# Token shift, wide products and low parts off GpSimd, PSUM banks freed earlier, and fewer small transfers in a two-layer GLA / MoBA / RWKV-7 step

## The chip, the cores and the metric

The kernel runs on one core of a Trainium2 chip. A core has four compute engines with an instruction queue each: TensorE (PE in the profile, with its weight loads as PEld), VectorE (DVE), ScalarE (ACT) and GpSimd (POOL). A fifth queue, SyncE (SP), only issues DMA transfers. Each queue runs in order and waits on semaphores. The metric is the device time of one execution in microseconds; lower is better.

## The reference

Two layers of a hybrid decoder trunk run on 256 prompt tokens and 8 single-token samples (264 columns in all), with 1024 features. Per layer:

```python
gq, gk, gv, g_low, g_out, mq, mk, mv, pr, pg = split_cols(x @ p['w_in'], IN_SPLITS)
# GLA branch: chunked linear attention, gated with silu(g_out)
# MoBA branch: rotary on mq, mk; softmax attention over own and cached blocks
prev = jnp.concatenate([shift0[:, None, :], pr[:, :-1]], axis=1)      # RWKV-7 branch: token shift
ps = pr + p['rwkv_mu'] * (prev - pr)
r, k7, v7, w_low, a_low, gr_low = split_cols(ps, RWKV_SPLITS)
...
k7 = k7 * (1.0 + (a - 1.0) * p['rwkv_k_a'])
yw, wkv_S = rwkv7_scan(r, w, k7, v7, kk, a, wkv_S0)                   # done in chunks of 64 tokens
...
merged = sum over branches of sigmoid(pg + b_gate) * (branch @ w_branch)
x = layer_norm(ALPHA * x + merged @ p['w_out'], ln1_g, ln1_b)
h = jnp.square(relu(x @ p['w_up'])) @ p['w_down']
x = layer_norm(ALPHA * x + h, ln2_g, ln2_b)
```

The caches and recurrent states are returned as well.

## The kernel before

Activations lie feature-major: 128 features on the partitions, 264 tokens along a row, 8 such row tiles for the 1024 features. All dense weights stream through in 146 chunks of 512 KB per layer (`Weights`, L206 to L241). A chunk is loaded into one of three staging tiles (`st`) from the SP queue; ACT casts it to a reduced-precision high part `wh`, DVE subtracts to get the low part `wl` (`split`, L200 to L202). `unit` (L283) takes one chunk and issues 24 matmuls of 128x264: high by high, high by low, low by high. So PE needs from ACT and DVE two casts and two subtractions of 128x512 for each 24 matmuls. `next` cuts a chunk two units ahead of its use and asks for loads further ahead.

In a layer the units run in this order: the RWKV projections `pr` (14 row tiles, collected in four groups `prp`, then shifted by `tok_shift` into `pst`, L643), GLA's `gq gk gv go`, MoBA's `mq mk` with rotary (`rope`, L1280) and `mv`, the gates and branch products for GLA, RWKV and MoBA, then `w_out` with LN1, 32 units of `w_up`, and `w_down` with LN2. The three branches are Python generators (`rwkv`, `gla`, `moba`, and `samples` for the RWKV sample states) that are advanced between units, so that their small work stands between the dense matmuls. The order on each engine is then fixed at build time by a scheduler with a simulated timeline; at run time each queue follows that order and waits where it must.

Places and names that the change and the prediction touch:

- `tok_shift(g)` (L643 to L653): GpSimd forms the difference of neighbouring columns of `prp` for a whole group (128x1024), DVE applies `mu` and adds, row by row.
- `rwkv`: `k7` gets its affine part on DVE (L713) and its product with `kx` on GpSimd (L718); `bk` and `qr` (decayed keys and queries, L741 to L745) are half DVE, half GpSimd. `parts` (L603) makes high and low parts of `rk` and `ys`, the low part on GpSimd (L606).
- `Dg` to `Mb` and `Tb` to `TZ`: 16x16 diagonal blocks are inverted with blocks on partitions. Two transposing round trips through DRAM re-arrange them: `md` (write L766, eight reads L769) and `td` (write L883, sixteen reads L887). PE's products `y` (L900) need `Zt`, which is made from `TZ` (L896). `S<-in_wkv` (L824) are two loads of the samples' states, `sa` (PE) reads them.
- `emit_go` (L1273 to L1276) gates GLA's output: ACT's tanh and a DVE product read the PSUM bank of the unit. `rope` (L1280 to L1292): ACT copies the bank to SBUF, then three ACT and one DVE copy of 32 partitions read the bank again, crosswise. Ordinary units have two PSUM banks in turn, so a bank that is held delays the unit after the next.
- `LayerNorm`: `prepare` scales the residual with alpha (L418), `add` adds the products. After LN1's statistics (`rs`, L505) early `w_up` units, computed without normalisation, are fixed up: DVE `u` (L479), GpSimd `u * rs` (L481), ACT relu (L1523), GpSimd square (L1525). Mode "keep" (LN1) also writes the normalised rows `s` for the next residual: GpSimd subtracts `mu` (L515) and multiplies by `rs` (L519), DVE applies gain and bias (L520), and later ACT multiplies by alpha (L418).
- `quad` (L185): a set of small matmuls of which the last is issued first, the others after it.

Of the kernel before, what the change touches and what calls it, by code (L numbers as in the profile page):

```python
# [10 lines left out]
F32 = mybir.dt.float32  # L11
# [10 lines left out]
NS = 8  # L22
# [89 lines left out]
def kernel(ctx: ExitStack, tc: tile.TileContext, i, o, depth):  # L112
# [72 lines left out]
    def quad(products):  # L185

        out, l, r, start, stop = products[-1]
        head = PE.matmul(out, l, r, start=start, stop=stop).ins
        with tc.issue_after(head):
            for out, l, r, start, stop in products[:-1]:  # L190
                mm(out, l, r, start, stop)
# [13 lines left out]
    class Weights:  # L205
# [27 lines left out]
        def next(self):  # L233
            c = self.used
            self.used += 1
            ahead = NWP // 2 - 1
            self.cut_to(c + ahead)
            self.load_to(c + ahead + NST)
            return self.pc.pop(c)
# [158 lines left out]
    class LayerNorm:  # L398
# [16 lines left out]
        def prepare(self, m):  # L415
            s = self.s[ALL, m]
            if isinstance(self.x, Rows):
                A.mul(s, s, alpha)  # L418
            else:
                A.mul(s, self.x.h.f32(m), alpha)  # L420
                V.scalar_tensor_tensor(s, self.x.l.f32(m), alpha, s, op0=OP.mult, op1=OP.add)
            if m > 2:
                G.tensor_tensor(s, s, self.k, op=OP.subtract)

        def add(self, m, ps):
            s = self.s[ALL, m]
            V.tensor_tensor(s, s, ps, op=OP.add)
# [63 lines left out]
        def normalise(self):  # L491
# [15 lines left out]
            if self.mode == "keep":  # L507
                for _ in range(16):
                    yield
            if self.mode == "split":  # L510
                self.xh, self.xl = Rows(KT, "xh", F32R), Rows(KT, "xl", F32R)
            for k in range(KT):
                s = self.s[ALL, k]
                e = G if self.mode == "keep" or k % 2 else V
                e.tensor_tensor(s, s, mu, op=OP.subtract)  # L515
                if self.mode == "keep":
                    yield
                    yield
# [31 lines left out]
    for l in range(depth):  # L550
# [11 lines left out]
        ka1 = lpool.tile([128, 4], F32, tag="ka1", name="ka1")  # L562
        SP.dma_start(shift0, i["shift0"][l])
# [27 lines left out]
        V.tensor_scalar(ka1, P("k_a", 0, 4), -1.0, 1.0, op0=OP.mult, op1=OP.add)  # L591
        if l == 0:
            make_idx()

        if True:
# [48 lines left out]
            def tok_shift(g):  # L644
# [4 lines left out]
                G.tensor_sub(d[:, :, 0:T], pr[:, :, 0:T], pr[:, :, 1:T + 1])  # L649
                G.tensor_sub(d[:, :, T:N], shift0[:, 4 * g:4 * g + n, :], pr[:, :, T + 1:N + 1])  # L650
                for j in range(n):
                    V.scalar_tensor_tensor(d[:, j], d[:, j], P("mu", 4 * g + j), pr[:, j, 1:N + 1], op0=OP.mult, op1=OP.add)
                G.tensor_copy(sho[:, 4 * g:4 * g + n, :], pr[:, :, T:N + 1])  # L653

            def rwkv():
# [56 lines left out]
                for m in range(4):  # L712
                    V.tensor_scalar(k7[:, m], a7[:, m], P("k_a", m), ka1[:, m:m + 1], op0=OP.mult, op1=OP.add)  # L713
# [20 lines left out]
                for hf in range(2):  # L734
# [9 lines left out]
                    G.tensor_tensor(bt[:, :, :, 64:128], v4(k7), Pi[:, hs], op=OP.mult)  # L744
                    G.tensor_tensor(qt[:, :, :, 64:128], v4(r7), Pd[:, hs, :, 1:65], op=OP.mult)  # L745
# [19 lines left out]
                md = dr.tile([8, 16, 16, 16], F32, tag="md", name="md")  # L765
                SP.dma_start(md.rearrange("b i q j -> (b i) (q j)"), Dg.rearrange("r c p j -> r (c p j)"))  # L766
# [115 lines left out]
                td = dr.tile([8, 16, 2, 16, 16], F32, tag="td", name="td")  # L882
                SP.dma_start(td.rearrange("b q z i j -> (b q) (z i j)"), Tb.rearrange("q z i j -> q (z i j)"))  # L883
# [70 lines left out]
                def pre_chunk(c):  # L954
# [3 lines left out]
                          for p in range(4) for f in HALF for h2 in range(2)])  # L958
# [142 lines left out]
            def gla():  # L1101
# [74 lines left out]
                for tt in range(2):  # L1176
# [4 lines left out]
                      for tt in range(2) for m in range(2) for a in range(2) for h2 in range(2)])  # L1181
# [128 lines left out]
            def moba():  # L1310
# [113 lines left out]
                for m in range(4):  # L1424
                    ex = []
                    pss = [bank([128, 384], "qkT") for _ in range(2)]
                    for a in range(4):
                        keys = slice(0, 128) if a < 2 else slice(0, 256)
                        cols = slice(0, 128) if a < 2 else slice(128, 384)
                        for h2 in range(2):  # L1430
                            f = HALF[h2]
                            mm(pss[h2][HALF[a % 2], cols], mq[f, m, 64 * a:64 * a + 64], mk[f, m, keys])
# [200 lines left out]
```

## Time and profile before

Three runs took 1155.83 to 1157.29 us, median 1156.64 us. One execution was profiled:

| | |
|---|---|
| time of the profiled execution | 1157.98 us |
| its span (first to last instruction) | 1156.2 us |
| PE busy / weight loads | 1086.6 us (94%) / 1014.7 us (88%) |
| DVE busy | 882.3 us (76%) |
| ACT busy | 662.0 us (57%) |
| POOL busy | 534.8 us (46%) |
| mean granted TensorE clock | 0.982 |
| DMA, mean | 166 GB/s |

Busy is the union of the spans of an engine's instructions. Matmuls overlap each other, so a busy PE may still be short of its best rate. An idle time is shown with the work whose end ended it. The granted clock is 1.00 at 2.4 GHz and 0.50 at 1.2 GHz.

### The profile page before, as it was taken

To read this page: it belongs to the slowest core of one execution; us is meant where nothing else is said; L and a number is where in the kernel's file an instruction comes from. 1 tells how busy PE (TensorE), PEld (TensorE's weight loads), DVE (VectorE), ACT (ScalarE), POOL (GpSimd) and SP (SyncE) were. 2 spreads that over 40 slices of the span, in tenths; PEclk is the share of its full clock that TensorE was granted. 3 is DMA by queue.
4 is the path that set the end of the run, shared out by engine and by line. 5 is a ranking of instruction groups with operands and counts; after the bars stand their busy time and mean duration, and the time that the engine had idled before them with its cause. 6 is when DMAs were issued, how large, how long until landed. Compare 5 with 4: busy or idle time off the path is not lost.

```text
span 1156.2 us, 26716 instructions
## 1 busy us (share of the span) xinstructions
PE 1086.6 (94%) x10284; PEld 1014.7 (88%) x10284; DVE 882.3 (76%) x1562; ACT 662.0 (57%) x1460; POOL 534.8 (46%) x633
## 2 busy tenths in 40 slices
PE   7998899999999899999989978899999998999996
PEld 7887788888999799999989867788789988999995
DVE  6898974668778998766799889555687888987554
ACT  5844444555766676655557645363567656766443
POOL 2373482460126875441265655714411377753412
PEclk9999999999999999999999989999999998999998
DMA  7445665474454455655534456645634544556661
GB/s 266 144 131 180 176 201 172 130 251 129 146 176 155 146 181 170 188 191 183 164 114 152 144 167 186 202 129 157 225 110 148 173 153 146 163 171 196 183 182 57
DMA packets 71520, 191.89 MB, mean 166 GB/s; under 512 B 21136, under 2 KB 23904, under 8 KB 71392
## 3 DMA queue, kind: packets, MB, share of 16 engines
q1 hardware_dynamic: 66240, 173.39, 47.9%
q0 software_dynamic: 5152, 16.79, 4.5%
q8 instruction: 81, 1.33, 0.5%
q14 instruction: 47, 0.39, 0.1%
HBM read 179.17 MB, written 8.88 MB: 163 GB/s over the span
## 4 chain that ended last, share of the span: by engine, by line
PE 74%; DVE 12%; issue 5%; DMA 4%; ACT 3%; SPq 1%; POOL 1%; DVEq 0%; ACTq 0%; POOLq 0%
PE ps L179 40%; PE psd L179 16%; PE psb L179 5%; DVE wl L202 4%; PE mn L179 1%; DVE s L520 1%; DMA kcache<-in_kcache,idx 1%; DMA TZ<-td 1%; DMA S<-in_wkv 1%; SPq L887 1%; ACT wh L201 1%; PE y L179 1%; PE w L183 1%; PE zy L179 1%; PE qkT L179 1%
## 5 line engine op out<-in xcount | busy, mean ns | idle before, releaser
L202 DVE TENSOR_TENSOR wl<-st,wh 128x512 fp32r<-128x512 f32 (+1 forms) x585 | 458.0, 795 | 162.2 <-ACT wh L201 155.2
L201 ACT CAST wh<-st 128x512 fp32r<-128x512 f32 (+1 forms) x585 | 354.5, 617 | 286.1 <-PE ps L179 134.0
L179 PE MATMUL ps<-xh,wh 128*128 128x264 f32 x904 | 269.4, 298 | 15.9 <-DVE go L1276 4.7
L179 PE MATMUL ps<-xl,wh 128*128 128x264 f32 x904 | 265.1, 293 | 1.8 <-DVE xl L202 1.8
L179 PE MATMUL ps<-xh,wl 128*128 128x264 f32 x904 | 264.3, 292 | 1.3 <-DVE wl L202 1.3
L179 PEld LDWEIGHTS ps<-xh,wh 128*128 128x128 f32 x904 | 174.8, 193 | 29.0 <-issue 5.5
L179 PEld LDWEIGHTS ps<-xl,wh 128*128 128x128 f32 x904 | 175.0, 194 | 6.9 <-issue 2.7
L179 PEld LDWEIGHTS ps<-xh,wl 128*128 128x128 f32 x904 | 174.9, 193 | 5.2 <-issue 2.8
L179 PE MATMUL ps<-ch,wh 128*128 128x266 f32 x600 | 174.5, 292 | 5.1 <-ACT wh L201 3.4
L179 PE MATMUL ps<-ch,wl 128*128 128x266 f32 x600 | 173.1, 290 | 6.0 <-DVE wl L202 5.9
L179 PE MATMUL ps<-cl,wh 128*128 128x266 f32 x600 | 173.4, 289 | 0.4 <-DVE cl L440 0.4
L179 PE MATMUL psd<-hh,wh 128*128 128x264 f32 x512 | 145.5, 284 | 0.0
L179 PE MATMUL psd<-hl,wh 128*128 128x264 f32 x512 | 145.3, 284 | 0.0
L179 PE MATMUL psd<-hh,wl 128*128 128x264 f32 x512 | 145.3, 284 | 0.0
L179 PEld LDWEIGHTS ps<-ch,wl 128*128 128x128 f32 x600 | 114.4, 191 | 8.1 <-DVE wl L202 7.9
L179 PEld LDWEIGHTS ps<-ch,wh 128*128 128x128 f32 x600 | 115.0, 192 | 6.6 <-ACT wh L201 3.9
L179 PEld LDWEIGHTS ps<-cl,wh 128*128 128x128 f32 x600 | 115.5, 193 | 0.9 <-DVE cl L440 0.8
L1496 POOL TENSOR_TENSOR acc<-acc,gt 128x264 f32<-128x264 f32 x32 | 35.2, 1102 | 147.8 <-DVE gt L1495 136.5
L481 POOL TENSOR_TENSOR u<-u,rs 128x264 f32<-128x264 f32 x75 | 79.2, 1056 | 37.5 <-DVE u L479 35.8
L179 PEld LDWEIGHTS psd<-hh,wh 128*128 128x128 f32 x512 | 96.4, 188 | 0.0
L179 PEld LDWEIGHTS psd<-hl,wh 128*128 128x128 f32 x512 | 96.3, 188 | 0.0
L179 PEld LDWEIGHTS psd<-hh,wl 128*128 128x128 f32 x512 | 96.3, 188 | 0.0
(598 smaller groups left out, 2167.9 us busy)
## 6 DMA issues: line engine op xcount, KB each, us to landing
st<-in_w SPq DMA_DIRECT2D x291, 512.0 KB, 3.6
S<-in_wkv SPq DMA_DIRECT2D x4, 512.0 KB, 4.8
gS<-in_gla SPq DMA_DIRECT2D x8, 256.0 KB, 5.6
out_wkvs<-S SPq DMA_DIRECT2D x4, 512.0 KB, 3.3
out_glas<-gS SPq DMA_DIRECT2D x8, 256.0 KB, 5.5
out_k<-mk SPq DMA_DIRECT2D x2, 528.0 KB, 3.7
out_v<-mv SPq DMA_DIRECT2D x2, 528.0 KB, 3.5
out_y<-s SPq DMA_DIRECT2D x8, 132.0 KB, 1.7
```

The source lines that it names most:

```text
L179: PE.matmul(out, l, r, start=start, stop=stop)
L183: PE.matmul(out, l, r, start=start, stop=stop, skip_group_check=True)
L201: A.copy(hi, src)
L202: V.tensor_sub(lo, src, hi.bitcast(F32))
L481: G.tensor_tensor(u, u, self.rs, op=OP.mult)
L520: V.tensor_scalar(s, s, self.P(self.gn, k), self.P(self.bn, k), op0=OP.mult, op1=OP.add)
L887: SP.dma_start(TZ[16 * b:16 * b + 16, z], td[b, :, z].rearrange("q i j -> i q j"))
L1496: G.tensor_tensor(acc[ALL, m], acc[ALL, m], gts[e], op=OP.add)
```

## The change

Per layer:

1. `tok_shift`: with omu = 1 - mu, the shift becomes mu * prev + omu * pr. ACT scales the neighbour columns row by row (14 operations of 128x256), DVE adds the rest (14, as before), GpSimd only copies the eight sample columns (the state is scaled with mu at the layer's start).
2. `k7`'s affine part goes from DVE to ACT, its product with `kx` from GpSimd to DVE; the GpSimd halves of `bk` and `qr` go to DVE; the low parts in `parts` go to DVE.
3. `emit_go`: ACT also takes half of the bank's value to SBUF, one DVE operation then works from SBUF. `rope`: all four crosswise copies are ACT's and read the SBUF copy.
4. LN1 "keep": gain, bias and alpha are folded (`ag`, `nag`, `ab`): two DVE operations per row tile, none on GpSimd, and no scaling by ACT in LN2's `prepare`.
5. `md` and `td`: the write makes a layout from which one read (`Mb`) and two reads (`TZ`) suffice, instead of eight and sixteen.
6. `next` asks for loads one chunk less far ahead.
7. `quad` can issue two leading matmuls, one for each of two banks; used for `mn`, `gA` and MoBA's `qkT`.

```diff
-    def quad(products):
-        out, l, r, start, stop = products[-1]
+    def quad(products, heads=1):
+        out, l, r, start, stop = products[-heads]
         head = PE.matmul(out, l, r, start=start, stop=stop).ins
+        for out, l, r, start, stop in products[len(products) - heads + 1:]:
+            with tc.issue_after(head):
+                head = PE.matmul(out, l, r, start=start, stop=stop).ins
...
-            self.load_to(c + ahead + NST)
+            self.load_to(c + ahead + NST - 1)
...
             if self.mode == "keep":
+                mr = T1([128, N], "mr")
+                V.tensor_tensor(mr, mu, rs, op=OP.mult)
                 for _ in range(16):
                     yield
+                for k in range(KT):
+                    s = self.s[ALL, k]
+                    V.scalar_tensor_tensor(s, s, ag[:, k:k + 1], rs, op0=OP.mult, op1=OP.mult)
+                    yield
+                    V.scalar_tensor_tensor(s, mr, nag[:, k:k + 1], s, op0=OP.mult, op1=OP.add)
+                    yield
+                return
...
-                A.copy(hi, src)
-                G.tensor_tensor(lo, src, hi.bitcast(F32), op=OP.subtract)
+                split(src, hi, lo)
...
-                G.tensor_sub(d[:, :, 0:T], pr[:, :, 0:T], pr[:, :, 1:T + 1])
-                G.tensor_sub(d[:, :, T:N], shift0[:, 4 * g:4 * g + n, :], pr[:, :, T + 1:N + 1])
                 for j in range(n):
-                    V.scalar_tensor_tensor(d[:, j], d[:, j], P("mu", 4 * g + j), pr[:, j, 1:N + 1], op0=OP.mult, op1=OP.add)
+                    A.mul(d[:, j, 0:T], pr[:, j, 0:T], P("mu", 4 * g + j))
+                G.tensor_copy(d[:, :, T:N], shift0[:, 4 * g:4 * g + n, :])
+                for j in range(n):
+                    V.scalar_tensor_tensor(d[:, j], pr[:, j, 1:N + 1], omu[:, 4 * g + j:4 * g + j + 1], d[:, j], op0=OP.mult, op1=OP.add)
...
-                    V.tensor_scalar(k7[:, m], a7[:, m], P("k_a", m), ka1[:, m:m + 1], op0=OP.mult, op1=OP.add)
+                    A.activation(k7[:, m], a7[:, m], AF.Identity, scale=P("k_a", m), bias=ka1[:, m:m + 1])
...
-                G.tensor_tensor(k7, k7, kx, op=OP.mult)
+                V.tensor_tensor(k7, k7, kx, op=OP.mult)
...
-                    G.tensor_tensor(bt[:, :, :, 64:128], v4(k7), Pi[:, hs], op=OP.mult)
-                    G.tensor_tensor(qt[:, :, :, 64:128], v4(r7), Pd[:, hs, :, 1:65], op=OP.mult)
+                    V.tensor_tensor(bt[:, :, :, 64:128], v4(k7), Pi[:, hs], op=OP.mult)
+                    V.tensor_tensor(qt[:, :, :, 64:128], v4(r7), Pd[:, hs, :, 1:65], op=OP.mult)
...
-                for b in range(8):
-                    SP.dma_start(Mb[16 * b:16 * b + 16], md[b].rearrange("i q j -> q i j"))
+                SP.dma_start(Mb, md.rearrange("q b i j -> (q b) i j"))
...
-                for b in range(8):
-                    for z in range(2):
-                        SP.dma_start(TZ[16 * b:16 * b + 16, z], td[b, :, z].rearrange("q i j -> i q j"))
+                for z in range(2):
+                    SP.dma_start(TZ[:, z], td[z].rearrange("q b i j -> (b i) q j"))
...
-                    V.tensor_scalar(s, s, 0.5, 0.5, op0=OP.mult, op1=OP.add)
-                    V.tensor_tensor(go[:, j], s, ps, op=OP.mult)
+                    A.mul(go[:, j], ps, 0.5)
+                    V.scalar_tensor_tensor(go[:, j], s, 1.0, go[:, j], op0=OP.add, op1=OP.mult)
...
-                    (V.tensor_copy if q == 3 else A.copy)(u[d], ps[e])
+                    A.copy(u[d], t[e, m])
```

The scheduler makes a new order from this. Three places of it follow.

POOL in layer 0, at the end of LN1: before, with `a`, `sq` the last sums of the statistics, `s` the row tiles, `u` the fix of an early unit and `hr` its square.

```order
L449 TENSOR_TENSOR sq<-sq 128x264
L450 TENSOR_TENSOR a_5006<-a_5006,s 128x264
L515 TENSOR_TENSOR s<-s,mu 128x264 x8
L481 TENSOR_TENSOR u<-u,rs 128x264
L519 TENSOR_TENSOR s<-s,rs 128x264 x8
L481 TENSOR_TENSOR u<-u,rs 128x264
```

And after the change:

```order
L453 TENSOR_TENSOR sq<-sq 128x264
L454 TENSOR_TENSOR a_5002<-a_5002,s 128x264
L485 TENSOR_TENSOR u<-u,rs 128x264
L1539 TENSOR_TENSOR hr<-hr 128x264
L485 TENSOR_TENSOR u<-u,rs 128x264
```

The sixteen operations on `s` no longer stand around the first fix on POOL.

DVE at the same place: before, from the reciprocal that gives `rs` to the third `u`.

```order
L505 RECIPROCAL rs<-rs 128x264
L202 TENSOR_TENSOR wl<-st,wh 128x512 x4
L479 SCALAR_TENSOR_TENSOR u<-mu,wgb,ps 128x264
L202 TENSOR_TENSOR wl<-st,wh 128x512
L520 TENSOR_SCALAR s<-s,prm 128x264 x2
L202 TENSOR_TENSOR wl<-st,wh 128x512
L520 TENSOR_SCALAR s<-s,prm 128x264 x2
```

And after the change, where eight operations stand in one run:

```order
L509 RECIPROCAL rs<-rs 128x264
L205 TENSOR_TENSOR wl<-st,wh 128x512
L514 TENSOR_TENSOR mr<-mu,rs 128x264
L483 SCALAR_TENSOR_TENSOR u<-mu,wgb,ps 128x264
L205 TENSOR_TENSOR wl<-st,wh 128x512
L519 SCALAR_TENSOR_TENSOR s<-s,ag,rs 128x264 x8
L205 TENSOR_TENSOR wl<-st,wh 128x512
L483 SCALAR_TENSOR_TENSOR u<-mu,wgb,ps 128x264
L521 SCALAR_TENSOR_TENSOR s<-mr,nag,s 128x264 x3
L205 TENSOR_TENSOR wl<-st,wh 128x512
```

The low parts of the weights (`wl`) stand later among them: the third is behind the run of eight.

SP in layer 0 at the first round trip: before, `md` is the blocks' DRAM copy, `S` the states, `st` weights.

```order
L766 DMA md<-Dg 128x256
L824 DMA S_1041<-in_wkv 128x1024
L215 DMA st<-in_w 128x1024
L769 DMA Mb<-md 16x16x16 x8
L824 DMA S_1043<-in_wkv 128x1024
```

And after the change:

```order
L842 DMA S_1051<-in_wkv 128x1024
L218 DMA st<-in_w 128x1024
L785 DMA md<-Dg 128x16x16
L218 DMA st<-in_w 128x1024
L842 DMA S_1053<-in_wkv 128x1024
L787 DMA Mb<-md 128x256
```

Both loads of `S` stand ahead of the read of `md`, which is one transfer now.

## Rows read from the trace of the kernel before

**Rows 1.** Busy time by stage (columns: stretch, length, busy and count by engine, clock, DMA).

```profile
30.00:150.00 120.00, 106.50 (x951) 96.64 (x950) 104.67 (x186) 64.07 (x134) 59.59 (x72) 0.95 0.54 163
356.00:405.00 49.00, 43.69 (x336) 41.81 (x335) 44.45 (x60) 30.39 (x70) 40.42 (x44) 0.99 0.46 146
405.00:571.00 166.00, 166.00 (x1344) 166.00 (x1345) 128.44 (x191) 98.17 (x216) 75.68 (x82) 0.99 0.58 181
580.00:750.00 170.00, 146.28 (x1448) 131.80 (x1447) 148.22 (x258) 91.95 (x202) 105.44 (x134) 0.97 0.53 164
```

**Rows 2.** What PE waited for: us in total, times, longest.

```profile
PE ps L179 <- DVE wl L202: 7.2, 8, 1.4
PE y L179 <- DVE Zt L896: 7.0, 2, 3.8
PE ps L179 <- DVE go L1276: 4.7, 1, 4.7
...
PE ps L179 <- DVE rsn L1287: 3.9, 2, 1.9
PE sa L188 <- DMA S<-in_wkv: 3.6, 2, 2.8
PE ps L179 <- ACT wh L201: 3.4, 2, 1.7
PE m L179 <- DVE qr L742: 2.6, 4, 0.8
PE ps L179 <- ACT prp L310: 2.2, 2, 2.0
```

**Rows 3.** Two stretches with the clock halved, and one at full clock (columns as Rows 1).

```profile
107.50:110.90 3.40, 3.40 (x15) 1.74 (x16) 2.41 (x9) 0.61 (x1) 1.36 (x2) 0.50 0.89 301
...
670.70:677.50 6.80, 5.62 (x25) 5.62 (x26) 6.54 (x13) 0.62 (x1) 3.38 (x4) 0.50 0.43 109
...
500.00:503.40 3.40, 3.40 (x30) 3.40 (x29) 3.02 (x5) 1.24 (x2) 3.40 (x4) 1.00 0.50 160
```

**Rows 4.** DVE in order of time: start, length, operation, and idle time before it.

```profile
46.96 2.47 DVE L591 TENSOR_SCALAR ka<-prm 128x4 f32<-128x4 f32 x1
...
385.02 1.80 DVE L505 RECIPROCAL rs<-rs 128x264 f32<-128x264 f32 x1 [1.43 <-ACT rs L501]
...
667.47 3.42 DVE L762 TENSOR_SCALAR Dg<-Mt,cst 128x256 f32<-128x256 f32 x1
```

**Rows 5.** Groups by form: count, busy us, mean ns, idle us before.

```profile
L1287 DVE COPY rsn<-ps 32x264 f32<-32x264 f32 x16 | 6.9, 431 | 2.2 <-ACT rsn L1287 1.7
L718 POOL TENSOR_TENSOR k<-k,pst 128x1056 f32<-128x1056 f32 x2 | 6.9, 3434 | 12.1 <-DVE k L713 12.1
...
L773 DVE SCALAR_TENSOR_TENSOR rk<-pst,prm,k 128x264 f32<-128x264 f32 x8 | 3.4, 480 | 0.0
...
L201 ACT CAST xh<-s 128x264 fp32r<-128x264 f32 x8 | 3.1, 410 | 3.3 <-DVE s L520 3.3
...
L741 DVE TENSOR_TENSOR bk<-b,Pi 128x512 f32<-128x512 f32 x4 | 3.1, 766 | 0.0
```

**Rows 6.** DMA issues of SP in order of time, layer 0.

```profile
99.32 3.78 SPq L769 DMA_DIRECT2D Mb<-md  x8
103.20 0.39 SPq L824 DMA_DIRECT2D S<-in_wkv  x1
...
132.37 10.57 SPq L887 DMA_DIRECT2D TZ<-td  x16
```

**Rows 7.** All 32 reads of `td` (L887): issue to landing.

```profile
DMA to landing us min/median/max: 1.8/2.8/5.8
```

**Rows 8.** POOL in order of time, end of LN1 in layer 0.

```profile
382.70 6.67 POOL L515 TENSOR_TENSOR s<-s,mu 128x264 f32<-128x264 f32 x8 [2.90 <-ACT mu L498]
...
390.50 7.76 POOL L519 TENSOR_TENSOR s<-s,rs 128x264 f32<-128x264 f32 x8
398.22 0.80 POOL L481 TENSOR_TENSOR u<-u,rs 128x264 f32<-128x264 f32 x1
```

More of the change, by code (lines that the diff above doesn't have):

```diff
@@ L183, in group @@
         PE.matmul(out, l, r, start=start, stop=stop, skip_group_check=True)
-    def quad(products):
-        out, l, r, start, stop = products[-1]
+    def quad(products, heads=1):
+        out, l, r, start, stop = products[-heads]
         head = PE.matmul(out, l, r, start=start, stop=stop).ins
+        for out, l, r, start, stop in products[len(products) - heads + 1:]:
+            with tc.issue_after(head):
+                head = PE.matmul(out, l, r, start=start, stop=stop).ins
         with tc.issue_after(head):
-            for out, l, r, start, stop in products[:-1]:
+            for out, l, r, start, stop in products[:-heads]:
                 mm(out, l, r, start, stop)
@@ L416, in prepare @@
             s = self.s[ALL, m]
-            if isinstance(self.x, Rows):
-                A.mul(s, s, alpha)
-            else:
+            if not isinstance(self.x, Rows):
                 A.mul(s, self.x.h.f32(m), alpha)
@@ L426, in add @@
             s = self.s[ALL, m]
-            V.tensor_tensor(s, s, ps, op=OP.add)
+            if isinstance(self.x, Rows):
+                V.scalar_tensor_tensor(s, ps, ab[:, m:m + 1], s, op0=OP.add, op1=OP.add)
+            else:
+                V.tensor_tensor(s, s, ps, op=OP.add)
             if m == 0:
@@ L513, in normalise @@
                 s = self.s[ALL, k]
-                e = G if self.mode == "keep" or k % 2 else V
+                e = G if k % 2 else V
                 e.tensor_tensor(s, s, mu, op=OP.subtract)
-                if self.mode == "keep":
-                    yield
-                    yield
                 e.tensor_tensor(s, s, rs, op=OP.mult)
@@ L562 @@
         ka1 = lpool.tile([128, 4], F32, tag="ka1", name="ka1")
+        omu = lpool.tile([128, 14], F32, tag="omu", name="omu")
+        ag, nag, ab = (lpool.tile([128, KT], F32, tag=n_, name=n_) for n_ in ("ag", "nag", "ab"))
         SP.dma_start(shift0, i["shift0"][l])
@@ L591 @@
         V.tensor_scalar(ka1, P("k_a", 0, 4), -1.0, 1.0, op0=OP.mult, op1=OP.add)
+        V.tensor_scalar(omu, P("mu", 0, 14), -1.0, 1.0, op0=OP.mult, op1=OP.add)
+        G.tensor_tensor(shift0, shift0, P("mu", 0, 14)[:, :, None].to_broadcast([128, 14, NS]), op=OP.mult)
+        V.tensor_scalar(ag, P("ln1_g", 0, KT), alpha, None, op0=OP.mult)
+        V.tensor_scalar(nag, P("ln1_g", 0, KT), -alpha, None, op0=OP.mult)
+        V.tensor_scalar(ab, P("ln1_b", 0, KT), alpha, None, op0=OP.mult)
         if l == 0:
@@ L764, in rwkv @@
                     V.scalar_tensor_tensor(Dg, Mt[:, :, :, 16 * k:16 * k + 16], C("rm", k, k + 1), Dg, op0=OP.mult, op1=OP.add)
-                md = dr.tile([8, 16, 16, 16], F32, tag="md", name="md")
-                SP.dma_start(md.rearrange("b i q j -> (b i) (q j)"), Dg.rearrange("r c p j -> r (c p j)"))
+                md = dr.tile([16, 8, 16, 16], F32, tag="md", name="md")
+                SP.dma_start(md.rearrange("q b i j -> (b i) q j"), Dg.rearrange("r c p j -> r (c p) j"))
                 Mb = T1([128, 16, 16], "Mb")
-                for b in range(8):
-                    SP.dma_start(Mb[16 * b:16 * b + 16], md[b].rearrange("i q j -> q i j"))
+                SP.dma_start(Mb, md.rearrange("q b i j -> (q b) i j"))
                 rk = slot([128, 4, N], "rk")
@@ L957, in pre_chunk @@
                     quad([(psm[h2][f, p], bk[p // 2][HALF[h2], p % 2, c, f], qr[p // 2][HALF[h2], p % 2, c], True, True)
-                          for p in range(4) for f in HALF for h2 in range(2)])
+                          for p in range(4) for f in HALF for h2 in range(2)], 2)
                     for h2 in range(2):
@@ L1180, in gla @@
                        qd[HALF[h2], m, tt * 128:(tt + 1) * 128], True, True)
-                      for tt in range(2) for m in range(2) for a in range(2) for h2 in range(2)])
+                      for tt in range(2) for m in range(2) for a in range(2) for h2 in range(2)], 2)
                 for h2 in range(2):
@@ L1426, in moba @@
                     pss = [bank([128, 384], "qkT") for _ in range(2)]
[L1427 to L1432, printed above, removed]
+                    part_ = ((slice(0, 128), slice(0, 128)), (slice(128, 384), slice(0, 256)))
+                    quad([(pss[h2][HALF[a], cols], mq[HALF[h2], m, 128 * b + 64 * a:128 * b + 64 * a + 64], mk[HALF[h2], m, keys], True, True)
+                          for b, (cols, keys) in enumerate(part_) for a in range(2) for h2 in range(2)], 2)
                     for h2 in range(2):
```

4 lines of the change are left out of this document (2 added, 2 removed).

## The prediction

> **What bounds the kernel now.** I read the busy times by stage first, then what PE waited for, then the granted clock, then the queues of the engines that PE waited for. The stages are of two kinds [rows 1]. In 405 to 571 us (most of `w_up` and all of `w_down`) PE is busy all the time, with DVE at 128 and POOL at 76 of 166 us: whatever the change saves on other engines there is worth nothing. In 30 to 150 us (the in-projection of layer 0) PE is idle 13.5 us of 120 while DVE is busy 104.7; in 580 to 750 us, the same stage of layer 1, PE is idle 23.7 of 170 while DVE is busy 148.2; and in 356 to 405 us, around LN1, idle 5.3 of 49 with DVE at 44.5 and POOL at 40.4. So the time to be won lies where PE waits for DVE's queue or for things that stand behind it.
>
> PE's waits say for what [rows 2]: `Zt` (the second DRAM round trip) 7.0 us, `go` 4.7, the rotary's `rsn` 3.9, the states' DMA `S` 3.6, the weights' `wh` 3.4, `qr` 2.6 and `wl` 7.2. Of the eight waits for `wl` half the time lies in the first units of layer 1, behind the LN2 fix that the change leaves alone; I count 3.2 us as open to the change. Together 28.4 us, both layers.
>
> There is a second price behind each longer wait. The granted clock is 0.50 in eight stretches of 3.4 or 6.8 us, and there PE gets through 15 matmuls in 3.4 us instead of 30 [rows 3]. Each of the eight begins where a wait of PE ends: at 56.3, 107.5, 128.0, 148.5, 404.5, 670.7, 735.6 and 974.5 us. The first follows the wait for `prp`, which the change does not address. The other seven (five of 3.4, two of 6.8 us, 30.6 us in all) follow waits for `S`, `rsn`, `Zt`, LN1, `go`, `Zt` and LN1 again. Half of their length is lost, 15.3 us.
>
> **Why DVE is late.** DVE's busy time is not all work. A scale of 128x4 values takes 2.47 us at 46.96 us, and one of 128x256 takes 3.42 us at 667.47 us [rows 4]: each runs while POOL is in a wide product (the `k7` product of 3.43 us, the low part of `rk`) and ends with it. That second wait is what holds `go` and with it PE for 4.7 us. The change takes the `k7` product [rows 5], the token shift's differences, the `bk`/`qr` halves and the low parts away from POOL.
>
> The Trainium skill, "SBUF — State Buffer", section "SBUF: two separate sides", says that DVE and GpSimd share one pair of SBUF ports under an exclusive lock, and that a DVE operation with two SBUF inputs holds it too. The trace agrees with the first half (2.47 us for 128x4). The second half speaks against the change: the moved products still hold the pair on DVE. By it the gain is POOL's time less DVE's for the same product, 3.43 against some 1.6 us for `k7`, and not POOL's whole time.
>
> **The change part by part.**
>
> *Wide products, token shift.* DVE gets per layer the `k7` product (128x1056, twice the 0.766 us of a 128x512 product [rows 5], 1.5 to 1.9 us), four `bk`/`qr` halves (3.1 us) and two low parts (some 3.2 us, one of them late in the layer). It loses four scales of `k7` (1.6 us at 0.41), four steps of `go` (about 1.6) and eight rotary copies (3.4 us at 0.431 [rows 5]). So its own work stays within 2 us; what goes is the waiting for POOL. The two places of rows 4 alone are 5.5 us of it. PE sees it as the waits for `qr` 2.6, `go` 4.7 and 1.4 of `wl`.
>
> *ACT's price.* ACT gets per layer 14 scales of the token shift and four of `k7` (0.41 us each from SBUF [rows 5], 7.4 us), eight more rotary copies and four halvings of `go` (0.4 us each, 4.8 us), and loses eight alpha scales (3.4 us) where nobody waits. ACT is busy only 64 of 120 us in 30 to 150 us [rows 1], but that is uneven: PE's wait for `prp`, 2.2 us [rows 2], is a wait for ACT. The cost is between nothing and the whole 12 us per layer; nearest is the wait for `prp`, so I take 1 us per layer.
>
> *Rotary and `go`.* The unit's bank is freed by ACT's first one or two operations instead of after four more reads on two queues. The waits for `rsn`, 3.9 us, go; next in line is the unit's own copy, which PE does not wait for today.
>
> *Transfers.* Eight reads of `md` hold SP 3.78 us (0.47 per issue), and only then does the second `S` load go out, at 103.20 us, for which PE waits; the sixteen reads of `td` take 10.57 us [rows 6]. With one and two reads, and both `S` loads ahead of `Mb`, the states come over 3 us earlier in layer 0 and `TZ` is complete some 7 us earlier, if one transfer takes no longer than the small ones today, 1.8 to 5.8 us from issue to landing [rows 7]. That covers `S` (3.6) and `Zt` (7.0). What could be late next is the inversion's chain of small DVE steps ahead of it, which is why I do not count all. A load asked for one chunk later still has two units (about 6 us) to land; I price it at nothing, its cover being the two cut chunks ahead of PE.
>
> *LN1.* POOL's two runs on `s` (6.67 and 7.76 us) stand on either side of the first `u * rs`, and the second must wait until 398.22 us, 11.4 us after `rs` is there at 386.8 us [rows 4, 8]; relu, casts and `wh` stand behind it on ACT. PE's waits there are `wh` (3.4, both layers [rows 2]) and part of `wl`. After the change POOL is free for the fixes. DVE instead gets 17 operations, 8.2 us by the 480 ns row [rows 5], for eight that lose time behind POOL. In the new row the second `u` stands behind three `wl` (0.77 each by the product of that size [rows 5]), the first `u`, `mr` and the run of eight (0.48 each): 7.1 us after `rs`, so that its fix can start some 4 us earlier than today. The run of eight delays the third `wl` by 3.8 us; its cover is the two cut chunks that PE has in hand (some 6 us), and without them PE would wait that long once per layer. I count the LN1 waits as mostly gone.
>
> *The rest.* Leading matmuls per bank, no alpha scales, and the residual with the folded bias stand in stretches where PE is full or where no wait is shown: zero, with 1 us either way for a new order.
>
> **Sum.** Not every wait will go to nothing, since the next queue is not far behind: DVE's own work fills over four fifths of the in-projection. I take 70% of 28.4 us, 19.9, and 60% of the 15.3 us lost to the halved clock, 9.2; less 2 us for ACT. That is 27 us. The profiled execution took 1158.0 us, so 1131; it stands 1.3 us above the median of the runs, so 1130 us.
>
> **Rivals.**
>
> *All of it.* Every addressed wait and its half clock goes: 43.7 us, 1113 us. For it: the stages' other engines are below PE then. Against it: all queues run in order, and a new order has new waits. 15%.
>
> *Half.* The order, fixed by a simulated timeline, leaves PE waiting at the same points for work that is only a little earlier; DVE's base load stays the bound. 40% of the waits (11.4) and 30% of the clock (4.6), less 2: 14 us, 1143 us. For it: DVE 104.7 of 120 [rows 1]. 20%.
>
> *The round trips stay long.* The 64-byte runs of the transposing transfers are as many as before (2048 and 4096); if they, and not SP's issues, set the time, `Zt` stays: 7.0 times 0.7 and two half-clock stretches (2 us) are lost from the gain, 1137 us. Against it: `TZ` spreads over the 10.57 us of the issues [rows 6]. 10%. The Trainium skill, "DMA: Bandwidth & Descriptors", section "Why small descriptors are slow (HBM only)", gives each small packet a fixed price, by which merging the transfers would win nothing. The issue rows speak for the issues; no run here shows the merged form.
>
> *ACT takes DVE's place.* The 12 us per layer that ACT gains all stand in the in-projection, ahead of `wh` casts in an in-order queue. If half of that lands on PE (12 us in both layers) with four more half-clock stretches (7 us), and only LN1's 8 us is won, the time is 1157 + 11 = 1168 us. It decides from the point where PE's waits for ACT pass some 25 us. For it: the wait for `prp` at 56 us. Against: 64 of 120 [rows 1]. 10%.
>
> **How the numbers follow.** The forecast has 45%, its own range 1120 to 1140 us. With full (15%), half (20%), long trips (10%) and ACT (10%), 1111 to 1152 leaves out the lower part of the full case and the ACT case, about 18%. What this kernel's measurement can tell from no change is about 0.2%, 2.3 us. Faster by more: all but the ACT case and the weak end of the half, 87%; within: 5%; slower: 8%.
>
> **What would show it.** Right: PE's idle time in the two in-projection stretches falls by a third or more; waits for `rsn` and `go` are gone; `Mb` and `TZ` land within 3 to 6 us of one or two issues; no 2 us operation of 128x4 on DVE; fewer than eight half-clock stretches. Wrong: PE waits for `prp` or `wh` with ACT full; `y` still waiting for `Zt`; `wl` late behind the run of eight at LN1.

## Result and the profile after

The changed kernel took 1136.97 us (median of four runs, 1133.49 to 1138.12) against 1156.24 us before: a ratio of 0.9831, 95% interval 0.9811 to 0.9851. It is 19.3 us faster; the forecast was 26.6 us faster, with 1111 to 1152 us as its range. The profiled execution took 1137.04 us, its span 1135.3 us. The page gives PE 1077.8 us busy (1086.6 before), so PE's idle time fell from 69.6 to 57.5 us.

To see where, I cut the span at dense units that both kernels run alike (the first matmul of the 64th, 80th, ... of the 292 units). Four stretches hold all of the gain: the in-projection and branches of layer 0 (units 0 to 64), LN1 and the first part of `w_up` (80 to 120), and the same of layer 1 (152 to 216, 216 to 264). The views of busy time by stretch, first of the kernel before and then of the changed one:

```profile
4.10:318.20 314.10, 297.11 (x3155) 263.82 (x3155) 234.77 (x468) 175.88 (x390) 130.69 (x170) 0.98 0.55 176
366.60:494.90 128.30, 122.99 (x967) 121.20 (x966) 112.65 (x171) 83.84 (x202) 85.77 (x94) 0.99 0.56 171
590.20:908.60 318.40, 292.24 (x3164) 259.67 (x3164) 243.18 (x484) 180.69 (x403) 144.12 (x174) 0.98 0.51 160
908.60:1061.20 152.60, 147.26 (x1159) 145.12 (x1158) 132.57 (x202) 99.73 (x234) 96.49 (x105) 0.98 0.53 164
```

```profile
4.20:304.40 300.20, 290.63 (x3155) 257.19 (x3156) 220.69 (x464) 186.62 (x419) 111.44 (x160) 0.99 0.59 183
352.90:479.90 127.00, 121.35 (x966) 119.75 (x966) 111.91 (x182) 80.70 (x194) 72.43 (x78) 1.00 0.56 172
575.30:888.90 313.60, 294.20 (x3164) 258.11 (x3164) 233.04 (x475) 191.62 (x433) 120.39 (x161) 0.98 0.54 163
888.90:1040.20 151.30, 144.60 (x1159) 142.72 (x1158) 132.31 (x210) 95.66 (x225) 84.33 (x89) 1.00 0.53 164
```

The first pair of numbers is the stretch and its length, the next PE's busy time. Layer 0's in-projection won 13.9 us, layer 1's only 4.8, LN1 1.3 in either layer. What PE waited for in the changed kernel (us in total, times, longest), beside [rows 2]:

```profile
PE ps L179 <- DVE wl L205: 9.2, 6, 2.1
...
PE y L179 <- DVE Zt L913: 3.8, 2, 2.3
PE sa L188 <- DMA S<-in_wkv: 3.7, 1, 3.7
PE op L179 <- DMA R<-Rl: 3.2, 4, 1.5
PE ss L188 <- DMA kcache<-in_kcache,idx: 2.8, 2, 2.1
PE ps L179 <- ACT prp L313: 2.4, 5, 0.9
PE go L183 <- DVE Tb L896: 2.3, 1, 2.3
...
PE ps L179 <- ACT wh L204: 1.4, 2, 1.1
...
PE ps L179 <- ACT go L1292: 0.9, 1, 0.9
PE m L179 <- DVE qr L761: 0.9, 2, 0.5
```

`rsn` and DVE's `go` are gone, `qr` fell from 2.6 to 0.9. `Zt` fell only from 7.0 to 3.8. `S` is as long in total, but not in the same place: layer 0's wait of 2.8 us went, and layer 1's grew from 0.8 to 3.7. `wl` rose from 7.2 to 9.2; 7.2 of it now stand around the two LN1 and 2.0 in the first units of layer 1, where it was 3.7. So the waits that the prediction added up to 28.4 us (with the 3.2 of `wl` that it left open to the change) are 17.9 us now: 37% went, where it took 70%. Of half clock there are four stretches, against eight (both without one behind PE's last matmul); beside [rows 3]:

```profile
131.90:135.20 3.30, 3.30 (x31) 2.97 (x31) 2.78 (x9) 0.00 (x0) 3.30 (x6) 0.54 1.01 391
671.60:674.90 3.30, 3.30 (x17) 1.40 (x21) 2.89 (x6) 0.25 (x1) 2.54 (x4) 0.50 0.54 217
709.10:712.40 3.30, 3.30 (x15) 3.19 (x15) 2.58 (x8) 0.49 (x2) 3.30 (x4) 0.50 1.07 337
828.30:834.60 6.30, 5.60 (x14) 3.76 (x15) 5.05 (x18) 3.21 (x12) 0.00 (x0) 0.52 0.12 47
```

The number behind POOL's busy time and count is the granted clock; the windows are cut on tenths of a microsecond and lie a little inside the stretches. The four are 17.0 us long in all (three of 3.4, one of 6.8), against 34.0 before, so at half their length 8.5 us less was lost to them (forecast 9.2). Three of the four lie in layer 1, and the last is new: it stands around a wait of 1.3 us of small products (`zg`) at the end of the RWKV branch.

At LN1 the run of eight is where the prediction put it (DVE, and PE's row at the same place):

```profile
374.22 0.68 DVE L205 TENSOR_TENSOR wl<-st,wh 128x512 fp32r<-128x512 f32 x1
374.83 4.26 DVE L519 SCALAR_TENSOR_TENSOR s<-s,ag,rs 128x264 f32<-128x264 f32 x8
379.01 0.68 DVE L205 TENSOR_TENSOR wl<-st,wh 128x512 fp32r<-128x512 f32 x1
```

```profile
379.75 0.39 PE L179 MATMUL ps<-ch,wl 128*128 128x266 f32 x1 [2.06 <-DVE wl L205]
```

PE had used up its two cut chunks and stood 2.06 us. For `wl` it waits 3.6 us in this stretch, where before it waited 1.7 for `wh`, 1.1 for `wl` and 0.8 for `u`: the same 3.6 us under another name. In layer 1 it waits 3.6 for `wl` and 1.1 for `wh`, more than the 3.3 of before. What LN1 won is the half-clock stretch that no longer follows (3.4 us at half speed in layer 0, 6.8 in layer 1: 1.7 and 3.4 us).

The transfers of layer 1, in SP's timeline (start, us, engine, line, tiles):

```profile
659.43 0.38 SPq L785 DMA_DIRECT2D md<-Dg  x1
659.99 4.60 SPq L1243 DMA_DIRECT2D gS<-in_gla  x1
664.68 0.38 SPq L218 DMA_DIRECT2D st<-in_w  x1
665.12 0.42 SPq L842 DMA_DIRECT2D S<-in_wkv  x1
666.30 0.33 SPq L787 DMA_DIRECT2D Mb<-md  x1
...
693.49 0.51 SPq L901 DMA_DIRECT2D td<-Tb  x1
...
696.19 4.17 SPq L904 DMA_DIRECT2D TZ<-td  x2
```

and on the chain of waits:

```profile
659.43 6.84 DMA md<-Dg
666.30 5.51 DMA Mb<-md
```

The merged read of `Mb` lies within the forecast's 3 to 6 us (5.5). The two reads of `TZ` whose landing the trace has are slower (6.6 and 7.0 us from issue to landing), and so is this write of `md` (6.8 us; 2.7 at the same place before). In layer 1 the second `S` load still goes out late, behind one `gS` issue that held SP for 4.60 us, and PE waits for it.

### The profile page after: what moved, and what is told of

Same layout as the page of the kernel before. It is cut to its first block, busy times and chain, and to the rows that moved or that the text cites. A ratio compares the mean times of both kernels' runs of the same rounds, so it can differ in the third digit from the quotient of the medians.

```text
span 1135.3 us, 26669 instructions
## 1 busy us (share of the span) xinstructions
PE 1077.8 (95%) x10284; PEld 1002.6 (88%) x10284; DVE 857.8 (76%) x1570; ACT 676.9 (60%) x1503; POOL 466.4 (41%) x581
## 4 chain that ended last, share of the span: by engine, by line
PE 69%; DVE 10%; DMA 5%; issue 3%; ACT 2%; POOL 1%; SPq 0%; DVEq 0%; ACTq 0%; POOLq 0%
PE ps L179 36%; PE psd L179 16%; PE psb L179 5%; DVE wl L205 3%; DMA kcache<-in_kcache,idx 2%; DMA R<-Rl 1%; DVE s L521 1%; DMA out_wkvs<-S 1%; ACT wh L204 1%; DMA md<-Dg 1%; PE zy L179 1%; PE zg L179 1%; DVE cl L444 1%; PE pov L188 1%; PE w L183 1%
## 5 line engine op out<-in xcount | busy, mean ns | idle before, releaser
L205 DVE TENSOR_TENSOR wl<-st,wh 128x512 fp32r<-128x512 f32 (+1 forms) x585 | 440.2, 764 | 161.3 <-ACT wh L204 154.7
L179 PE MATMUL ps<-xh,wh 128*128 128x264 f32 x904 | 266.7, 295 | 10.1 <-ACT xh L204 4.5
L179 PE MATMUL ps<-xl,wh 128*128 128x264 f32 x904 | 262.2, 290 | 1.6 <-DVE xl L205 1.6
L179 PEld LDWEIGHTS ps<-xh,wh 128*128 128x128 f32 x904 | 172.4, 191 | 21.8 <-issue 7.1
L179 PEld LDWEIGHTS ps<-xl,wh 128*128 128x128 f32 x904 | 172.7, 191 | 7.5 <-issue 3.9
L179 PEld LDWEIGHTS ps<-xh,wl 128*128 128x128 f32 x904 | 172.6, 191 | 4.0 <-issue 1.8
L485 POOL TENSOR_TENSOR u<-u,rs 128x264 f32<-128x264 f32 x75 | 81.6, 1089 | 64.3 <-DVE u L483 60.9
```

Source lines behind the costliest of these rows:

```text
L205: V.tensor_sub(lo, src, hi.bitcast(F32))
L485: G.tensor_tensor(u, u, self.rs, op=OP.mult)
```

## Experiments

Theory at the start: the gain is PE no longer waiting behind DVE, which lost time beside GpSimd's wide products. Rivals: the transfers, LN1 or the banks carry it, or parts work only together. The first set ran beside a kernel before of 1156.4 us. The second and third set ran on other chips, on which the kernel before took 1184.1 and 1189.8 us; from chip to chip only ratios to it can be compared. Times are medians, intervals 95%.

**LN1 undone** (two DVE operations per row tile back to GpSimd's two and DVE's one, with ACT's alpha):

```diff
...
+                A.mul(s, s, alpha)
...
-                    V.scalar_tensor_tensor(s, s, ag[:, k:k + 1], rs, op0=OP.mult, op1=OP.mult)
-                    yield
-                    V.scalar_tensor_tensor(s, mr, nag[:, k:k + 1], s, op0=OP.mult, op1=OP.add)
...
-                e = G if k % 2 else V
+                e = G if self.mode == "keep" or k % 2 else V
                 e.tensor_tensor(s, s, mu, op=OP.subtract)
...
```

> The changed kernel with only the LN1 part undone (GpSimd subtracts and multiplies on s, DVE gain and bias, ACT's alpha scale, as before). The changed kernel took 1137 us. Theory A (the terms of the prediction): LN1's waits and its two half-clock stretches were worth 7 to 8 us, so this takes 1144 to 1145 us. Theory B (from the trace after): the run of eight only puts waits for wl (2.2, 1.7, 2.25, 1.6 us) where those for wh were, and the part is worth the 2.5 us by which the units around LN1 came faster: 1139 to 1140 us, with half-clock stretches after LN1 again. Theory C (no part is worth anything by itself, the new order as a whole is): anywhere within 5 us of 1137, below it too.

Measured: 1136.14 us, 0.9828 (0.9806 to 0.9850), no difference from the changed kernel. Theory A falls. By stretch, the two around LN1 are 1.6 us longer each (128.6 and 152.9 against 127.0 and 151.3 us), the old lengths, with the old waits and a half-clock stretch behind each (388.3 and 951.5 us), as theory B had it; but its 2.5 us do not show in the whole time, which is within theory C's 5 us. Layer 0's in-projection was 3.0 us shorter although PE's order there is the same, row for row: its half-clock stretch at 131.9 us is missing in this run. One run of a kernel thus differs from another by some 3 us there, and a part worth 3 us cannot be seen in the whole time.

**Transfers undone** (eight reads of `md`, sixteen of `td`):

```diff
...
-                for z in range(2):
-                    SP.dma_start(TZ[:, z], td[z].rearrange("q b i j -> (b i) q j"))
+                for b in range(8):
+                    for z in range(2):
+                        SP.dma_start(TZ[16 * b:16 * b + 16, z], td[b, :, z].rearrange("q i j -> i q j"))
```

> The changed kernel with only the two DRAM round trips as before (eight reads of md, sixteen of td). Theory A (prediction): S and Zt were 10.6 us of waits, 70% of it and three half-clock stretches depend on the transfers: 10 us, 1147 us, with PE waiting over 3 us for Zt in each layer and for S in layer 0. Theory B (trace after): PE still waits 3.7 us for S and 3.8 for Zt with merged transfers, so only some 3 us and one or two stretches were won: 1141 to 1143 us. Rival (the round trips stay long whoever issues them): within 2 us of 1137.

Measured: 1134.96 us, 0.9829 (0.9810 to 0.9848). No difference either. SP's timeline of this kernel in layer 0:

```profile
121.11 0.52 SPq L902 DMA_DIRECT2D td<-Tb  x1
...
125.23 9.88 SPq L906 DMA_DIRECT2D TZ<-td  x16
```

The `td` trip did become shorter by merging: from the issue of `td` to the last landing of `TZ` it takes 15.7 and 13.4 us with sixteen reads, 10.2 and 10.2 with two. The `md` trip did so only in layer 0: up to the last landing of `Mb` it takes 11.8 and 11.6 us with eight reads, 8.5 and 12.4 with one. But the wait for `Zt` is 4.2 us with sixteen and 3.8 with two, so that its fall from 7.0 did not come from merging. The order fits this: with the long trip the scheduler puts the first `y` behind 30.7 and 182.3 dense units, with the short one behind 30.0 and 181.5. PE does dense work meanwhile either way; the shorter trip moved its consumer forward and left the wait. The time is the rival's; its reason, trips that stay long, does not hold for `td`.

**GpSimd undone** (token shift, `k7`, halves of `bk` and `qr`, low parts):

```diff
-                    V.tensor_tensor(bt[:, :, :, 64:128], v4(k7), Pi[:, hs], op=OP.mult)
+                    G.tensor_tensor(bt[:, :, :, 64:128], v4(k7), Pi[:, hs], op=OP.mult)
...
-                    A.mul(d[:, j, 0:T], pr[:, j, 0:T], P("mu", 4 * g + j))
+                G.tensor_sub(d[:, :, 0:T], pr[:, :, 0:T], pr[:, :, 1:T + 1])
...
```

> The changed kernel with the wide products back on GpSimd: token shift with its differences, the k7 product (its affine part on DVE), the bk and qr halves, the low parts. Theory A (DVE lost time beside GpSimd's wide work, and PE behind it): 8 to 12 us slower than the changed kernel, 1145 to 1149 us, 2 us operations of 128x4 on DVE again, PE waiting for qr, go or wl in both layers. Rival (ACT's 14 scales per layer cost what GpSimd's leaving gives): within 3 us of 1137, with fewer waits of PE for prp.

Measured: 1150.47 us, 0.9952 (0.9936 to 0.9969): 13.5 us slower than the changed kernel. Theory A holds, 1.5 us above its range, with an operation of 128x4 that takes 2.47 us and PE's waits for `qr` (3.6 us) and `wl` (10.4), but none for `go`. Both in-projections are longer, 306.8 and 323.5 us against 300.2 and 313.6:

```profile
3.90:310.70 306.80, 289.76 (x3163) 257.21 (x3164) 228.54 (x462) 182.04 (x404) 129.50 (x170) 0.99 0.57 181
580.40:903.90 323.50, 296.99 (x3164) 262.90 (x3163) 244.94 (x472) 184.85 (x415) 143.59 (x172) 0.96 0.51 158
```

Three timelines of this kernel at one place, POOL, DVE and PE:

```profile
640.18 1.19 POOL L762 TENSOR_TENSOR qr<-pst,Pd 128x512 f32<-128x512 f32 x1
641.33 1.29 POOL L761 TENSOR_TENSOR bk<-k,Pi 128x512 f32<-128x512 f32 x1
642.58 1.20 POOL L762 TENSOR_TENSOR qr<-pst,Pd 128x512 f32<-128x512 f32 x1
```

```profile
639.99 4.34 DVE L205 TENSOR_TENSOR wl<-st,wh 128x512 fp32r<-128x512 f32 x1
644.25 0.69 DVE L758 TENSOR_TENSOR bk<-b,Pi 128x512 f32<-128x512 f32 x1
644.87 0.77 DVE L759 TENSOR_TENSOR qr<-kk,Pd 128x512 f32<-128x512 f32 x1
```

```profile
645.69 0.51 PE L179 MATMUL m<-bk,qr 64*64 64x64 f32 x10 [1.81 <-DVE qr L759]
```

One `wl`, 0.68 us elsewhere, takes 4.34 us and ends half a microsecond after the last of three products that GpSimd runs back to back; DVE's `bk` and `qr` stand behind it, and PE behind them. In the whole trace 32 DVE operations last over 0.7 us longer than the fastest of their form, by 41.6 us together; in the changed kernel 18 do, by 17.2 us. DVE's busy time is 877.0 us here and 857.8 in the changed kernel, although more of the products are DVE's there. The Trainium skill, "SBUF — State Buffer", section "SBUF: two separate sides", says that DVE and GpSimd share a pair of ports under an exclusive lock for a whole instruction. The trace agrees, and here a run of GpSimd's products held DVE for the run and not for one of them; the same came in layer 0 (a step of the token shift, 4.11 us from 70.46 us). That is not always so. In the changed kernel small DVE steps beside a run of four (POOL, then DVE) are held for one operation each:

```profile
99.80 4.48 POOL L862 TENSOR_TENSOR S<-S,wS 128x512 f32<-128x512 f32 x4 [5.73 <-PE sa L179]
```

```profile
100.29 1.04 DVE L894 TENSOR_TENSOR tmp<-Mb,Tb 128x39 f32<-128x39 f32 x1
101.36 0.97 DVE L896 TENSOR_TENSOR Tb<-Tb,tmp 128x39 f32<-128x39 f32 x1
102.36 0.98 DVE L894 TENSOR_TENSOR tmp<-Mb,Tb 128x48 f32<-128x48 f32 x1
```

The experiment cannot tell DVE's freedom from another effect of the same edit, that the moved products take less time on DVE. The trace speaks for the first: with the products on GpSimd, DVE idles only 5.7 us for GpSimd's results, against 2.6 in the changed kernel, while the stretched operations differ by 24.4 us.

**GpSimd's part alone**: the kernel before with only this part changed.

> The kernel before with the GpSimd part alone (token shift, k7, bk and qr halves, low parts off GpSimd); LN1, transfers, go and rotary, loads and bank leads as before. Theory B (the gain is GpSimd leaving DVE's way, the other parts are worth nothing or less): as fast as the whole change or faster, 1130 to 1139 us, with no 2 us operation of 128x4 on DVE. Rival 1 (parts add up: undoing this part cost 13.5 us of 19.3): 1143 us. Rival 2 (the parts only work together, since each frees a queue that the others wait for): over 1147 us, and then the waits for Zt, S or rsn of the kernel before are still there at their old length.

Measured: 1168.66 us, 0.9877 (0.9845 to 0.9909), 1.2% faster than before, as undoing it cost 1.2%. Rival 1, the additive one, holds; theory B (the whole gain) and rival 2 fall.

**Banks undone** (go and the rotary copies read PSUM again):

```diff
-                    A.mul(go[:, j], ps, 0.5)
-                    V.scalar_tensor_tensor(go[:, j], s, 1.0, go[:, j], op0=OP.add, op1=OP.mult)
+                    V.tensor_scalar(s, s, 0.5, 0.5, op0=OP.mult, op1=OP.add)
+                    V.tensor_tensor(go[:, j], s, ps, op=OP.mult)
...
-                    A.copy(u[d], t[e, m])
+                    (V.tensor_copy if q == 3 else A.copy)(u[d], ps[e])
```

> The changed kernel with go and the rotary copies reading the PSUM bank again as before (DVE's product and one of four copies from the bank). Theory A: PE's waits for the rotary's rsn (3.9 us in both layers) and for go come back, with a half-clock stretch or two: 4 to 6 us slower, 1141 to 1143 us. Rival (the waits for rsn and go came from DVE being late behind GpSimd, which is still gone): no wait for rsn or go over 0.5 us and a time within 2 us of 1137.

Measured: 1130.16 us, 0.9780 (0.9765 to 0.9796), 6.8 us faster than the changed kernel, which neither theory had. And yet the waits came back:

```profile
PE ps L179 <- DVE go L1293: 4.4, 4, 1.9
...
PE ps L179 <- DVE rsn L1304: 3.6, 3, 2.9
```

In their place others are gone (`S` 3.7, `Tb` 2.3, half of `R`), and in layer 1's in-projection there is one half-clock stretch of 3.4 us instead of 13.6 us. That in-projection is 5.1 us shorter, as much as half of the 10.2 us less at half clock; PE's idle time in it is no less (20.6 against 19.4 us). Layer 0's is 1.6 us shorter.

**Rotary alone and go alone undone, leads undone.**

> The changed kernel with only the rotary copies as before (three on ACT and one on DVE, from the PSUM bank). Undoing go and rotary together made it 6.8 us faster. Theory P (four rotary copies of 0.4 us in a row on ACT, ahead of the casts wh, are the price): 1130 to 1132 us, and PE waits for rsn appear. Theory Q (it is go): within 2 us of 1137. Theory R (neither by itself; it is the placing of layer 1's states and round trip, which either edit may move): between, or both under 1134.

> The changed kernel with only go as before (two DVE operations, the product reading the PSUM bank). Theory P (the rotary copies are the price): within 2 us of 1137. Theory Q (the halving that ACT does per unit of go, and the DVE operation on SBUF behind it, are the price): 1130 to 1132 us. Theory R as said for the rotary copies.

> The changed kernel with loads asked for one chunk further ahead and with one leading matmul per set, as before. The prediction priced both at nothing: within 2 us of 1137. Rival (the four undone parts explain only some 7 of 19.3 us, so the rest sits here): 5 to 12 us slower, 1142 to 1149 us, with PE waits on small products or loads that the changed kernel lacks.

Measured: rotary 1161.95 us, 0.9809 (0.9774 to 0.9844); go 1166.77 us, 0.9848 (0.9818 to 0.9878); leads 1157.89 us, 0.9778 (0.9746 to 0.9811). The changed kernel was not run on that chip, so they are told apart from each other only: go is slower than leads. Which half of the banks' 6.8 us it was stays open. If the changed kernel's 0.9831 holds on that chip too, the rival for leads (5 to 12 us slower) falls.

**LN1 spread, and with it banks, and leads.** Each of the sixteen operations is issued only behind the newest `wl`:

```diff
...
-                    V.scalar_tensor_tensor(s, s, ag[:, k:k + 1], rs, op0=OP.mult, op1=OP.mult)
-                    yield
-                    V.scalar_tensor_tensor(s, mr, nag[:, k:k + 1], s, op0=OP.mult, op1=OP.add)
+                    with tc.issue_after(weights.last):
+                        V.scalar_tensor_tensor(s, s, ag[:, k:k + 1], rs, op0=OP.mult, op1=OP.mult)
+                    yield
+                    with tc.issue_after(weights.last):
+                        V.scalar_tensor_tensor(s, mr, nag[:, k:k + 1], s, op0=OP.mult, op1=OP.add)
```

> The changed kernel unaltered, as the control for the three others on their chip. On the first chip its ratio to the kernel before was 0.983; if that ratio holds on every chip it is 0.981 to 0.985 here. On the chip of the second set of runs PE lost 10 to 14 us that the profile puts down to nothing but issue, in runs of small products; if that chip comes again, its profile shows them too and the ratio may be as high as 0.987.

> The changed kernel with LN1's sixteen operations on s held behind the newest wl of the unit in which each is asked for, so that no run of eight stands ahead of a wl. Theory (the run of eight put waits for wl in the place of LN1's old ones): the waits of 2.2, 1.7, 2.25 and 1.6 us for wl go, 5 to 8 us faster than the control. Rival (PE waits there because ACT's casts stand behind the fixes, and wl is late anyway): wh or hh is waited for instead, within 2 us of the control.

> The kernel with LN1 spread, and go and rotary as before. Theory P (reading the banks through ACT costs ACT and DVE time where neither is free): 5 to 8 us faster than the kernel with LN1 spread alone, as undoing both gave 6.8 us on the first chip. Theory R (that 6.8 us came from where layer 1's small work happened to be placed, which any edit changes): within 3 us of it. If both edits hold: ratio 0.967 to 0.973 to the kernel before.

> As the one before, with loads one chunk further ahead and one leading matmul per set again. By the prediction (both priced at nothing): within 2 us of the kernel with LN1 spread and banks undone. By the ratio of the second set (0.978 with leads undone against 0.983): 5 us faster.

Measured on one chip: the changed kernel 1167.12 us, 0.9799 (0.9775 to 0.9823); LN1 spread 1149.63 us, 0.9668 (0.9636 to 0.9699); with banks undone too 1164.90 us, 0.9808 (0.9783 to 0.9832); with leads undone as well 1170.71 us, 0.9833 (0.9812 to 0.9855). The control's ratio agrees with the first chip's (0.9831) within the intervals. LN1 spread is 17.5 us faster than the changed kernel, twice and more what the theory allowed. The stretches around LN1 are 0.6 and 1.6 us shorter, although the waits of 2 us are gone (the longest for `wl` there is 0.5 in layer 0): DVE has the same work, and later units pay with four waits of up to half a microsecond. Layer 0's in-projection is 3.6 us longer, in the same order. All the rest is layer 1's in-projection, which the edit does not touch (first the changed kernel, then LN1 spread):

```profile
585.50:919.80 334.30, 306.12 (x3165) 267.67 (x3164) 233.41 (x475) 191.62 (x433) 120.22 (x161) 0.94 0.49 153
```

```profile
588.50:904.00 315.50, 294.83 (x3164) 260.42 (x3163) 233.18 (x475) 191.47 (x433) 121.08 (x162) 0.97 0.53 162
```

The same work in 18.8 us less, at a granted clock of 0.97 instead of 0.94: 17.0 us of it at half clock instead of 40.9, which is 12 us, and PE idle 20.7 us instead of 28.2. PE's order in layer 0's in-projection is the same in both; in layer 1's the scheduler, set off differently by LN1, placed the small products otherwise. Undoing the banks puts 16.7 us back in that stretch, where on the first chip it took 5.1 us away. So theory P falls, and theory R, whose bound of 3 us was far too narrow, is nearer: over all kernels and the three chips this stretch lasts 307.6 to 335.3 us (307.6 to 313.6 in the four kernels of the first chip that lack the wide products), while the dense units 64 to 80 and 120 to 152 take 47.4 to 48.5 and 95.1 to 95.4 us in every one of them. Leads undone is 5.8 us slower than banks undone alone, with intervals that overlap; neither expectation had that sign.

LN1 spread is the fastest kernel by ratio; it was run on that one chip only.

## Why the prediction was right or wrong

- *Direction and main cause*: right; the gain was forecast 7.3 us too large. GpSimd's wide products held DVE, and taking them away is worth 1.2% of the 1.7%, measured from both sides. No 128x4 operation of 2 us is left on DVE, and PE's idle time in the two in-projections fell by a third, from 43.2 to 29.0 us, which is a sign that the prediction named. Each side compares one order with another, and orders differ too: on the first chip the two in-projections together take 607 to 614 us in the four kernels without these products and 630 and 633 in the two with them, but on the third chip four kernels that all lack them take 630 to 653. So the effect stands clear of the orders seen on the first chip; its size may be off by some microseconds. The other 0.5% belongs to no part that was undone by itself.
- *The total is nearer than its terms, which is partly luck.* By the prediction's shares (70% of the waits, 60% of the half clock) its sum holds some 8 us for GpSimd's part, 10.5 for the transfers, 7 for LN1 and 4 for the rotary. Undone one by one, GpSimd's part was worth 13.5, transfers and LN1 nothing that can be seen, and the rotary with `go` less than nothing (6.8 us faster without them).
- *The half clock*: 9.2 us forecast, 8.5 by the same count in the profiled execution. One stretch came at a place that I had not listed. Two readings were too simple. Not each of the eight begins where a wait ends: those at 670.7 and 974.5 us begin inside one (it ends at 671.9 and 975.4). And half its length is not always what a stretch costs: with the banks undone each LN1 has one of 3.4 us that the changed kernel lacks, but one wait of 1.5 us for `wl` less, and takes as long (126.9 and 151.3 us against 127.0 and 151.3).
- *The waits, 70% of 28.4 us*: the term that was mis-sized. Less ACT's 2 us it was 17.9 us; PE's idle time fell by 12.1. Two steps of it failed:
  - "I count the LN1 waits as mostly gone": the waits for `wl` took their place, at the same length in layer 0; in layer 1 `wl` and `wh` together are 4.7 us, where `wl`, `wh` and `u` were 3.3. The prediction had named the price, 3.8 us without cover, and then counted on the two cut chunks. They were used up; [rows 2] already showed PE waiting for `wh` and `wl` there, which it does not do with chunks in hand.
  - "That covers `S` (3.6) and `Zt` (7.0)": merged, `TZ` landed 5.4 and 3.2 us sooner after `td`, but `y` had been moved forward. `S` came early enough in layer 0, as forecast; in layer 1 it was still issued behind another load, since an issue can hold SP for over 4 us (4.60) with few transfers too.
- *ACT's price*: 2 us forecast. PE waits 2.4 us for `prp` instead of 2.2, and 0.9 for ACT's `go`: about 1 us. The rival of ACT in DVE's place did not come.
- *Round trips stay long* (1137 us, the time that came): that this time came is luck. The `td` trip, on which that rival rests, did become shorter, and undoing the transfers changed nothing. That I took the small reads' 1.8 to 5.8 us for the merged one was wrong (6.6 to 7.0). The Trainium skill, "DMA: Bandwidth & Descriptors", section "Why small descriptors are slow (HBM only)", gives each packet a fixed price, which spoke for long trips. The trace agrees so far that a merged read of `TZ`, eight times a small one, takes longer than a small one; the chain from `td` to the last landing became shorter all the same (10.2 us against 13.4 and 15.7).
- *Rotary, go, leads priced from their waits or at nothing*: open. The waits of `rsn` and `go` went with the change and returned without it, but the time moved with layer 1's in-projection, with either sign. That its order is the reason is not shown by itself.

## What to carry to other kernels

Where a simulated timeline makes the order, as here, a wait of PE shows where plan and chip differ. Shortening the work behind it can move the consumer forward instead of ending the wait (the `td` trip), so add up what an engine really gets rid of (DVE's operations stretched beside GpSimd). Cut the span at work that is the same in all kernels before comparing parts: pure `w_up` units repeated within 0.3 us in 95, and one in-projection differed by 18.8 us for an edit made elsewhere, on one chip. When a stretch varies like that, try several orders and keep the best, and do not read the sign of a small edit from one of them.

## What the runs showed that I had not expected

On the chips of the second and third set PE stands still, mostly in runs of small products, without anything to wait for that the profile shows. The changed kernel's timeline there (idle time and its end in brackets):

```profile
769.16 0.37 PE L183 MATMUL yc<-MN,UV 128*64 128x64 f32 x5 [0.40 <-issue]
770.62 0.35 PE L183 MATMUL yc<-MN,UV 128*64 128x64 f32 x4 [1.09 <-issue]
772.08 0.48 PE L183 MATMUL yc<-MN,UV 128*64 128x64 f32 x4 [1.11 <-issue]
```

Such waits come to 10 to 14 us in the four kernels of the second set, to 16.6 us in this trace and to none in the changed kernel's first trace; among them begins the longest stretch at half clock, 13.7 us from 771.0 us. The two traces of the same program, in the same order of PE's work in both in-projections, differ by 30.9 us. PE's idle time is 15 us longer in this one, and it has 47.7 us of half clock against 17.0, which is another 15 us: that accounts for 1137 us on one chip and 1167 on the other. What holds the issue was not tried, and stays open.
